# Four-layer hybrid encoder: a norm's squares summed on TensorE inside the first unit of the next stage

## The chip, the cores and the metric

The kernel runs on one core of a Trainium2 chip. The metric is the device time of one execution in microseconds (us). Shown of before are three runs and one profiled execution. The engines are named as the profile names them: PE is TensorE's matmul, PEld its weight load, DVE is VectorE, ACT is ScalarE, POOL is GpSimd, SP the queue that issues the weight transfers.

## The reference, cut to what matters

256 tokens of width 1024 pass four layers, each a mixer and an MLP, with a norm ahead of both and one at the end. The mixers are a state-space mixer (layers 0 and 3, called mix0 and mix3), a dilated attention (mix1) and a differential attention (mix2).

```python
def rmsnorm(x, g):
    y = x * rsqrt(mean(x * x, axis=-1, keepdims=True) + 1e-6)
    return y * g
for i in range(4):
    x = x + mixer[i](rmsnorm(x, norm_mix_g[i]), ...)
    h = rmsnorm(x, norm_mlp_g[i])
    x = x + square(relu(h @ mlp_w1[i])) @ mlp_w2[i]
out = rmsnorm(x, final_norm_g)
# differential attention, per head: softmax(a) - lambda * softmax(b), with
# lambda = exp(sum(l0 * l1)) - exp(sum(l2 * l3)) + lam_init
```

The factor of the norm, r = rsqrt(mean + eps), is one number per token; g is one number per channel. A projection of rmsnorm(x) is thus the projection of x * g, scaled by r for each token.

## The kernel before, in words

The activations lie transposed: `xT` has 8 tiles of 128 channels by 256 tokens. Every weight chunk (128 x 1024 numbers) comes by a transfer on SP into `raw`, is rounded by ACT (`whi`, line 110) and its rest taken by DVE (`wlo`, line 112). Activations are kept as such pairs too, and `mm3` (lines 149 to 151) makes each product of three matmuls: whi with the high part, whi with the low part, wlo with the high part. A "unit" is one projection of 256 columns: 48 matmuls of 128 x 256, in two halves of 24, one for each weight chunk.

At the end of a stage, `finish(n)` adds each of the eight finished tiles to `xT` (line 1151), and `norm_tile` makes the next stage's input of it: `norm_split` gives x * g as a pair (`uh`, `ul`; lines 232 and 233, tile `spl`), and `norm_square` squares the tile on ACT (lines 241 and 244). POOL adds the first seven squares to `sqacc` (line 246). `sums` (line 274) then adds over the channels by matmuls with one moving column (`guard`): the squares are the stationary operand, once for each half of the tokens, for `sqacc`, for the eighth square, and for a column of ones that carries eps. That is 6 products, and the trace shows each as two instructions, 12 in all. `rsqrt` is seven small DVE operations (lines 260 to 265); `bcast_tok` spreads r over a tile `rbc` (DVE line 282, a matmul, ACT line 284). All this is `norm_finish`.

`normalised` then multiplies `xT` by g and r and splits the result (`nf` or `nt`, `nh`, `nl`; lines 304 to 306), 8 tiles each.

Where the norm is used:
- The MLP works on `uh`, `ul` and scales by `rbc` as a unit leaves PSUM (line 349). `norm_finish("a3")` is written after `up(0)`, the first 96 matmuls.
- Each mixer calls `norm_finish("a0")` and `normalised` in `start`, ahead of its first unit. The first two units of mix0 and mix3, the first three q/k units of mix1 (`defer=3`) and the first q and k of mix2 work on `uh`, `ul` and are scaled behind (lines 460, 798, 983, tile `qkt`); all other units, the v chunks and `dt_unit` work on `nh`, `nl`.
- mix1's and mix2's `start` also clear key tiles by POOL (`kl`, line 136; lines 767, 772, 773), and mix2's `start` computes lambda (lines 943 to 951, with a matmul at line 945).
- `final` calls `sums` after everything else; PE has transposed the scaled output tiles (`final_tile`, line 1102) by then.

In `load` four pairs of squares are made by ACT (line 197) and added by DVE (line 201).

The order is set by a scheduler at build time: each engine has one fixed list, made from the order in which the program is written, priorities, and the scheduler's own idea of durations. The mixers write out their units by due times (`E(t, fn)`). `shifted("hi")` and `shifted("lo")` put the two conversions of a weight chunk back in priority by amounts set for each stage (`TUNE`).

Of the kernel before, what the change touches and what calls it, by code (L numbers as in the profile page):

```python
# [16 lines left out]
P = 128  # L17
# [7 lines left out]
NSPL = 12  # L25
NRAW = 5
CH = 1024
# [3 lines left out]
def classes(t):  # L31

    return t.rearrange("p (j c) -> p c j", c=4)

# [11 lines left out]
class Prog:  # L46
    def __init__(self, ctx, tc, aps, parts):
# [6 lines left out]
        self.ap_ = ep("small")  # L54
        self.sp = ep("sp")
# [77 lines left out]
    def lo_keys(self, name):  # L133

        t = self.lp.tile([P, 2, T], F32R, name=name)
        self.nc.gpsimd.memset(t[64:128].bitcast(F32), 0.0)
        return t

# [15 lines left out]
    def load(self, g, perm):  # L154
# [13 lines left out]
        for n, v in ((1, EPS / P), (D, 1.0 / D), (8 * D, 0.125 / D)):  # L168
            self.guard[n] = self.const.tile([P, 1], F32, name=f"guard{n}")
            nc.vector.memset(self.guard[n], v)  # L170
        self.ident = self.V("ident", 0, P)
# [22 lines left out]
        for c, b in enumerate(banks):  # L194
            nc.vector.tensor_copy(out=self.xT[:, 2 * c:2 * c + 2, :], in_=b)
            q = self.lp.tile([P, 2, T], F32, name=f"sq{c}")
            nc.scalar.activation(out=q, in_=b, func=AF.Square)
            if c == 0:
                sq = q
            else:  # L200
                nc.vector.tensor_tensor(out=sq, in0=sq, in1=q, op=ALU.add)
        self.sqs = [sq[:, 0, :], sq[:, 1, :]]
# [33 lines left out]
    def norm_square(self, j):  # L236
        nc = self.nc
        x = self.xT[:, j, :]
        if j == 0:
            self.sqs = [self.ap_.tile([P, T], F32, tag="sqacc", name="sqacc", bufs=2)]  # L240
            nc.scalar.activation(out=self.sqs[0], in_=x, func=AF.Square)
        else:
            sq = self.ap_.tile([P, T], F32, tag="sq", name="sq", bufs=3)
            nc.scalar.activation(out=sq, in_=x, func=AF.Square)  # L244
            if j < KD - 1:
                nc.gpsimd.tensor_tensor(out=self.sqs[0], in0=self.sqs[0], in1=sq, op=ALU.add)  # L246
            else:
                self.sqs.append(sq)

    def norm_tile(self, j, g, perm=False):  # L250
        if g is not None:
            self.norm_split(j, g, perm, self.xT[:, j, :])
        self.norm_square(j)

    def rsqrt(self, v, n):
# [3 lines left out]
        y, w, q = t("y"), t("w"), t("q", I32)  # L259
# [8 lines left out]

    def sums(self, bank, tiles, count):

        cols = [(self.ones, self.guard[1])] + [(t, self.guard[count]) for t in tiles]
        for i, (t, v) in enumerate(cols):
            for h in range(2):
                self.nc.tensor.matmul(bank[:, h:h + 1], lhsT=t[:, 0:P] if i == 0 else t[:, h * P:(h + 1) * P], rhs=v,
                                      start=i == 0 and h == 0, stop=i == len(cols) - 1, skip_group_check=True)

    def bcast_tok(self, r, scale, bank, out):
# [5 lines left out]
        nc.tensor.matmul(bank[:, 256:512], lhsT=self.ones, rhs=dg, start=True, stop=True)  # L283
        nc.scalar.copy(out=out, in_=bank[:, 256:512])

    def norm_finish(self, tag="r0"):
        nc = self.nc
        bank = self.bank(tag)
        self.sums(bank, self.sqs, D)
        r = self.rsqrt(bank[:, 0:2], 2)  # L290
        self.rbc = self.ap_.tile([P, T], F32, tag="rbc", name="rbc", bufs=2)
        self.bcast_tok(r, 1.0, bank, self.rbc)

    def normalised(self, g_mix, perm=False, keep=False):

        nc = self.nc
        nh, nl = (self.lp.tile([P, KD, T], F32R, name=n) for n in ("nh", "nl"))
        self.nf = self.lp.tile([P, KD, T], F32, name="nf") if keep else None
        rbc = classes(self.rbc) if perm else self.rbc
        for k in range(KD):  # L300
            x = classes(self.xT[:, k, :]) if perm else self.xT[:, k, :]
            t = self.nf[:, k, :] if keep else self.lp.tile([P, T], F32, tag="nt", name="nt", bufs=2)
            tv = t.rearrange("p (c j) -> p c j", c=4) if perm else t
            nc.vector.scalar_tensor_tensor(out=tv, in0=x, scalar=g_mix[:, k:k + 1], in1=rbc, op0=ALU.mult, op1=ALU.mult)
# [20 lines left out]
    def mlp(self, l, finish):  # L325
# [78 lines left out]
    def ssd_events(self, l, finish):  # L404
# [12 lines left out]
        def start():  # L417
            self.norm_finish("a0")
            st["n"] = self.normalised(gvec("g_mix", 8 * l, 8), keep=any(n[0] != "o" for n in cfg["native"]))
# [9 lines left out]
        def unit(kind, c0, defer):  # L429
# [227 lines left out]
        def r2():  # L657
            bank = self.bank("r2")

            self.sums(bank, [st["sq"][:, n, :] for n in range(2)], 8 * D)  # L660
            r = self.rsqrt(bank[:, 0:2], 2)
# [67 lines left out]

    def bias_rows(self):  # L730
# [19 lines left out]
    def dil_events(self, l, finish):  # L750
# [7 lines left out]
        cj = lambda t: t.rearrange("p (c j) -> p c j", c=4)  # L758

        def start():  # L760
            self.norm_finish("a0")
            st["rbp"] = lp.tile([P, T], F32, name="rbp")
            nc.scalar.copy(out=cj(st["rbp"]), in_=classes(self.rbc))
            st["n"] = self.normalised(self.V("g_mix", 8 * l, 8), perm=True)
            for i in range(2):
                st["bias", i] = lp.tile([P, 2, 514], F32, name=f"bias{i}")
                nc.gpsimd.memset(st["bias", i][:, :, 258:514], -1e30)
                st["kl", i] = self.lo_keys(f"kl{i}")
                for g in range(1, 3):
                    st["k", i, g] = [lp.tile([P, 2, T], F32R, name=f"k{i}{g}{q}") for q in range(2)]  # L770
                    for t in st["k", i, g]:
                        nc.gpsimd.memset(t[0:64, 1, :].bitcast(F32), 0.0)
                        nc.gpsimd.memset(t[64:128, 0, :].bitcast(F32), 0.0)
# [10 lines left out]
        def qk(hp, g, defer):  # L784
            b = self.bank(f"r{st.setdefault('rot', 0) % 2}")
            st["rot"] += 1
            nh, nl = (self.uh, self.ul) if defer else ([t[:, k, :] for k in range(KD)] for t in st["n"])
            for w in range(2):
                wh, wl = self.take((l, "qk", hp, g, w))
                o = b[:, w * T:(w + 1) * T]  # L790
                for k in range(KD):
                    c = slice(k * P, (k + 1) * P)
                    self.mm3(o, wh[:, c], wl[:, c], nh[k], nl[k], k == 0, k == 7)
                self.done()
            src = b.rearrange("p (w t) -> p w t", w=2)
            if defer:
                t = lp.tile([P, 2, T], F32, tag="qkt", name="qkt", bufs=2)
                nc.vector.tensor_tensor(out=t, in0=src, in1=st["rbp"].unsqueeze(1).to_broadcast([P, 2, T]), op=ALU.mult)
                src = t
# [17 lines left out]
        def vchunk(hp, i):  # L817
# [3 lines left out]
            nh, nl = st["n"]  # L821
# [450 lines left out]
```

## Time and profile before

| what | value |
|---|---|
| median of three runs | 1617.34 us (1616.33 to 1620.15) |
| the profiled execution | 1616.8 us, of which the span is 1615.0 us |
| PE busy | 1579.2 us (98%) |
| DVE, ACT, POOL busy | 1193.0, 959.2 and 133.1 us |
| mean transfer rate | 186 GB/s |

Stages by the trace, in us from the start of the span: load and the start of mix0 to about 45, mix0 to 245, mlp0 to 430, mix1 to 717, mlp1 to 900, mix2 to 1017, mlp2 to 1194, mix3 to 1426, mlp3 to 1606, the final norm to the end. [...]

### The profile page before, as it was taken

What the parts mean: (1) busy time and instruction counts of PE and PEld (TensorE: products, weight loads), DVE (VectorE), ACT (ScalarE), POOL (GpSimd) and SP (SyncE); (2) the same over time, 40 slices, a digit from 0 to 9 for tenths busy, and PEclk for the clock granted to TensorE, in tenths of its full rate; (3) what the DMA queues carried; (4) which work ended last, traced back from release to release, by engine and by line L of the source; (5) the groups of instructions that cost most, each with busy time, mean ns of one, the idle gap of its engine ahead of it and who ended that gap; (6) DMA issues with size and microseconds to landing.
All of it is one profiled execution on the core that took longest, in us unless ns stands there. A gap on an engine that the chain in (4) does not pass through costs nothing.

```text
span 1615.0 us, 32385 instructions
## 1 busy us (share of the span) xinstructions
PE 1579.2 (98%) x13018; PEld 1534.2 (95%) x13018; DVE 1193.0 (74%) x1996; ACT 959.2 (59%) x1627; POOL 133.1 (8%) x122
## 2 busy tenths in 40 slices
PE   8999999999999999999999999999999999999998
PEld 7989899999989999999999999999998898899997
DVE  6999998555776667666555899755578999985554
ACT  5577866444566666764444677644455777664444
POOL 0012131000200000010000100100010231310001
PEclk9999999999999999999999999999999999999999
DMA  6677765665565555546566575566656677656661
GB/s 210 216 217 235 218 198 177 214 212 188 150 172 166 166 158 168 161 132 200 184 186 190 157 216 151 173 197 191 191 161 183 211 219 226 214 176 190 193 194 65
DMA packets 230294, 299.84 MB, mean 186 GB/s; under 512 B 16496, under 2 KB 166256, under 8 KB 230144
## 3 DMA queue, kind: packets, MB, share of 16 engines
q1 hardware_dynamic: 209552, 262.51, 53.1%
q10 hardware_dynamic: 20592, 35.27, 7.6%
q8 instruction: 102, 1.67, 0.4%
q14 instruction: 48, 0.39, 0.1%
HBM read 296.41 MB, written 3.62 MB: 186 GB/s over the span
## 4 chain that ended last, share of the span: by engine, by line
PE 75%; DVE 13%; DMA 5%; ACT 3%; issue 2%; POOL 0%; SPq 0%; DVEq 0%; ACTq 0%; POOLq 0%
PE r L149 13%; PE r L151 13%; PE r L150 13%; PE a L149 8%; PE a L150 8%; PE a L151 8%; DVE wlo L112 3%; DMA raw<-in_ssd_in_w_dram 2%; PE r L147 2%; DMA bc<-scr 1%; PE a L829 1%; PE a L830 1%; PE a L828 1%; PE r L620 1%; ACT whi L110 1%
## 5 line engine op out<-in xcount | busy, mean ns | idle before, releaser
L112 DVE TENSOR_TENSOR wlo<-raw,whi 128x1024 fp32r<-128x1024 f32 (+1 forms) x490 | 591.3, 1214 | 301.6 <-ACT whi L110 299.9
L110 ACT CAST whi<-raw 128x1024 fp32r<-128x1024 f32 (+1 forms) x490 | 503.1, 1034 | 450.6 <-PE r L150 224.4
L151 PE MATMUL r<-spl,wlo 128*128 128x256 f32 x1248 | 352.1, 282 | 3.7 <-DVE wlo L112 3.7
L149 PE MATMUL r<-spl,whi 128*128 128x256 f32 x1248 | 353.5, 283 | 0.5 <-ACT whi L110 0.5
L150 PE MATMUL r<-spl,whi 128*128 128x256 f32 x1248 | 353.2, 283 | 0.4
L149 PE MATMUL r<-nh,whi 128*128 128x256 f32 (+1 forms) x1024 | 291.6, 285 | 6.7 <-DVE kl L142 3.2
L151 PE MATMUL r<-nh,wlo 128*128 128x256 f32 (+1 forms) x1024 | 286.9, 280 | 2.2 <-DVE wlo L112 2.2
L150 PE MATMUL r<-nl,whi 128*128 128x256 f32 (+1 forms) x1024 | 286.8, 280 | 0.0
L150 PE MATMUL a<-hl,whi 128*128 128x256 f32 x1024 | 286.0, 279 | 0.0
L149 PE MATMUL a<-hh,whi 128*128 128x256 f32 x1024 | 286.0, 279 | 0.0
L151 PE MATMUL a<-hh,wlo 128*128 128x256 f32 x1024 | 285.6, 279 | 0.0
L151 PEld LDWEIGHTS r<-spl,wlo 128*128 128x128 f32 x1248 | 238.5, 191 | 4.3 <-DVE wlo L112 4.1
L150 PEld LDWEIGHTS r<-spl,whi 128*128 128x128 f32 x1248 | 239.1, 192 | 1.3 <-DVE spl L233 1.1
L149 PEld LDWEIGHTS r<-spl,whi 128*128 128x128 f32 x1248 | 238.7, 191 | 1.1 <-ACT whi L110 0.7
L149 PEld LDWEIGHTS r<-nh,whi 128*128 128x128 f32 (+1 forms) x1024 | 193.4, 189 | 11.0 <-issue 6.1
L151 PEld LDWEIGHTS r<-nh,wlo 128*128 128x128 f32 (+1 forms) x1024 | 193.3, 189 | 3.2 <-DVE wlo L112 2.4
L150 PEld LDWEIGHTS r<-nl,whi 128*128 128x128 f32 (+1 forms) x1024 | 193.8, 189 | 0.7 <-DVE nl L306 0.2
L149 PEld LDWEIGHTS a<-hh,whi 128*128 128x128 f32 x1024 | 193.4, 189 | 0.2 <-ACT whi L110 0.2
L150 PEld LDWEIGHTS a<-hl,whi 128*128 128x128 f32 x1024 | 193.5, 189 | 0.0
L151 PEld LDWEIGHTS a<-hh,wlo 128*128 128x128 f32 x1024 | 192.4, 188 | 0.0
L246 POOL TENSOR_TENSOR sqacc<-sqacc,sq 128x256 f32<-128x256 f32 x48 | 43.3, 901 | 1100.8 <-ACT sq L244 1099.1
L595 ACT ACTIVATE e<-bc,tb 128x256 f32<-128x256 f32 (+1 forms) x256 | 95.5, 446 | 1.5 <-issue 1.5
(249 smaller groups left out, 2400.8 us busy)
## 6 DMA issues: line engine op xcount, KB each, us to landing
raw<-in_mlp_w_dram SPq DMA_DIRECT2D x256, 512.0 KB
raw<-in_ssd_in_w_dram SPq DMA_DIRECT2D x96, 512.0 KB
bc<-scr ACTq DMA_DIRECT2D x32, 768.0 KB
raw<-in_dil_qkv_w_dram SPq DMA_DIRECT2D x48, 512.0 KB
raw<-in_ssd_out_w_dram SPq DMA_DIRECT2D x32, 512.0 KB
raw<-in_dil_qkv_w_dram SPq DMA_DIRECT2D x64, 192.0 KB
raw<-in_diff_qkv_w_dram SPq DMA_DIRECT2D x24, 512.0 KB
raw<-in_dil_out_w_dram SPq DMA_DIRECT2D x8, 512.0 KB
```

Of the source, the lines that this page charges most:

```text
L110: self.nc.scalar.copy(out=hi[:, :n], in_=raw[:, :n])
L112: self.nc.vector.tensor_tensor(out=lo[:, :n], in0=raw[:, :n], in1=hi[:, :n].bitcast(F32), op=ALU.subtract)
L147: mm(out, lhsT=wh, rhs=xh, start=start, stop=stop, skip_group_check=True)
L149: mm(out, lhsT=wh, rhs=xh, start=start, stop=False, skip_group_check=True)
L150: mm(out, lhsT=wh, rhs=xl, start=False, stop=False, skip_group_check=True)
L151: mm(out, lhsT=wl, rhs=xh, start=False, stop=stop, skip_group_check=True)
L246: nc.gpsimd.tensor_tensor(out=self.sqs[0], in0=self.sqs[0], in1=sq, op=ALU.add)
L595: X = lambda o, i_, bias: nc.scalar.activation(out=o, in_=i_, func=AF.Exp, bias=bias)
L620: nc.tensor.matmul(b[(h % 2) * 64:(h % 2) * 64 + 64, n * T:(n + 1) * T], lhsT=xt[:, 1 - i, h * 64:(h + 1) * 64], rhs=G[h][:, i * T:(i + 1) ...
L828: mm(o, lhsT=nh[:, k, t], rhs=w_h, start=k == 0, stop=False)
L829: mm(o, lhsT=nh[:, k, t], rhs=w_l, start=False, stop=False)
L830: mm(o, lhsT=nl[:, k, t], rhs=w_h, start=False, stop=k == 7)
```

## The change

- `sums` loses the column of ones; eps is added by one more DVE operation on the two result columns. POOL's additions go: all eight squares go through `sums`, that is 16 products. Each of these matmuls is kept in program order, behind the PE instruction written before it; so is the matmul of `bcast_tok`.
- `norm_finish` is cut in two. `norm_sums` (matmuls and `rsqrt`) is written after the first 24 matmuls of a mixer's first unit, and after the first 48 of `up(0)` in an MLP; `norm_rows` (spreading r) after that unit.
- mix1 and mix2 have no `normalised` any more: all units work on `uh`, `ul`; q and k are multiplied by `rbc` as they leave PSUM, v by r with ACT's scale. mix0 and mix3 write `normalised` after the first unit; `dt_unit` works on `uh`, `ul`.
- Lambda is computed in mlp0, after the bias vectors. The key tiles are cleared within the first units.
- In `load`, squares are not added, and the conversions are not put back (`hi` and `lo` 0).
- `NSPL` goes from 12 to 16 (tiles for pairs), squares have 8 buffers for 3, a tile of 96 columns is left empty, the scratch for dynamic transfers is set to 4096.

```diff
     def sums(self, bank, tiles, count):
-        cols = [(self.ones, self.guard[1])] + [(t, self.guard[count]) for t in tiles]
-        for i, (t, v) in enumerate(cols):
+        for i, t in enumerate(tiles):
             for h in range(2):
-                self.nc.tensor.matmul(bank[:, h:h + 1], lhsT=t[:, 0:P] if i == 0 else t[:, h * P:(h + 1) * P], rhs=v, ...)
+                self.behind(self.nc.tensor.matmul(bank[:, h:h + 1], lhsT=t[:, h * P:(h + 1) * P], rhs=self.guard[count], ...))
+        v = self.ap_.tile([P, 2], F32, tag="ms", name="ms", bufs=2)
+        self.nc.vector.tensor_scalar(out=v, in0=bank[:, 0:2], scalar1=EPS, scalar2=None, op0=ALU.add)
+        return v
...
+    def behind(self, ins):
+        self.tc.keep_in_program_order(ins)
...
-    def norm_square(self, j):
+    def norm_square(self, j, perm):
         x = self.xT[:, j, :]
-            ...
-                nc.gpsimd.tensor_tensor(out=self.sqs[0], in0=self.sqs[0], in1=sq, op=ALU.add)
+        sq = self.ap_.tile([P, T], F32, tag="sq", name="sq", bufs=KD)
+        self.nc.scalar.activation(out=cj(sq) if perm else sq, in_=classes(x) if perm else x, func=AF.Square)
+        self.sqs.append(sq)
...
-    def norm_finish(self, tag="r0"):
+    def norm_sums(self, tag):
+        self.nbank = self.bank(tag)
+        self.r = self.rsqrt(self.sums(self.nbank, self.sqs, D), 2, "n")
+
+    def norm_rows(self):
+        self.rbc = self.ap_.tile([P, T], F32, tag="rbc", name="rbc", bufs=2)
+        self.bcast_tok(self.r, 1.0, self.nbank, self.rbc)
...
@@ mlp, up(s)
+                if s == 0 and j == 2:
+                    self.norm_sums("a3")
@@ mix0 and mix3, unit
                     self.done()
+                    if first and i == 0:
+                        self.norm_sums("a0")
+                if first:
+                    self.norm_rows()
                 evac(kind, c0, b.rearrange("p (n t) -> p n t", n=2), defer)
+                if first:
+                    st["n"] = self.normalised(gvec("g_mix", 8 * l, 8))
@@ mix1, qk
-            if defer:
-                t = lp.tile([P, 2, T], F32, tag="qkt", name="qkt", bufs=2)
-                nc.vector.tensor_tensor(out=t, in0=src, in1=st["rbp"]..., op=ALU.mult)
+                if first and w == 0:
+                    self.norm_sums("a0")
+                    fill(0)
+            if first:
+                self.norm_rows()
+            src = lp.tile([P, 2, T], F32, tag="qkt", name="qkt", bufs=2)
+            nc.vector.tensor_tensor(out=src, in0=b..., in1=self.rbc..., op=ALU.mult)
@@ final
-        self.sums(b, self.sqs, D)
-        r = self.rsqrt(b[:, 0:2], 2)
+        r = self.rsqrt(self.sums(b, self.sqs, D), 2)
```

More of the change, by code (lines that the diff above doesn't have):

```diff
@@ L24 @@
 NBUF = 5
-NSPL = 12
+NSPL = 16
 NRAW = 5
+GAP = 96
 CH = 1024
@@ L54, in __init__ @@
         self.ap_ = ep("small")
+        self.ap_.tile([P, GAP], F32, name="gap")
         self.sp = ep("sp")
@@ L167, in load @@
         self.guard = {}
-        for n, v in ((1, EPS / P), (D, 1.0 / D), (8 * D, 0.125 / D)):
+        for n, v in ((D, 1.0 / D), (8 * D, 0.125 / D)):
             self.guard[n] = self.const.tile([P, 1], F32, name=f"guard{n}")
             nc.vector.memset(self.guard[n], v)
+        self.lamt = self.const.tile([P, 6], F32, name="lamt")
         self.ident = self.V("ident", 0, P)
@@ L282, in bcast_tok, with normalised_tiles, normalised @@
             nc.vector.tensor_scalar(out=dg[:, b * P:(b + 1) * P], in0=self.ident, scalar1=r[:, b:b + 1], scalar2=scale, op0=ALU.mult, op1=ALU.mult)
-        nc.tensor.matmul(bank[:, 256:512], lhsT=self.ones, rhs=dg, start=True, stop=True)
+        self.behind(nc.tensor.matmul(bank[:, 256:512], lhsT=self.ones, rhs=dg, start=True, stop=True))
         nc.scalar.copy(out=out, in_=bank[:, 256:512])
-    def norm_finish(self, tag="r0"):
-        nc = self.nc
[L288 to L299, printed above, removed]
+    def norm_sums(self, tag):
[4 more added lines that the diff above has]
+        self.bcast_tok(self.r, 1.0, self.nbank, self.rbc)
+    def normalised_tiles(self, keep):
+        self.nhl = [self.lp.tile([P, KD, T], F32R, name=n) for n in ("nh", "nl")]
+        self.nf = self.lp.tile([P, KD, T], F32, name="nf") if keep else None
+    def normalised(self, g_mix):
+        nc = self.nc
+        nh, nl = self.nhl
         for k in range(KD):
[L301 to L304, printed above, removed]
+            t = self.nf[:, k, :] if self.nf is not None else self.lp.tile([P, T], F32, tag="nt", name="nt", bufs=2)
+            nc.vector.scalar_tensor_tensor(out=t, in0=self.xT[:, k, :], scalar=g_mix[:, k:k + 1], in1=self.rbc, op0=ALU.mult, op1=ALU.mult)
             nc.scalar.copy(out=nh[:, k, :], in_=t)
@@ L417, in start @@
         def start():
-            self.norm_finish("a0")
-            st["n"] = self.normalised(gvec("g_mix", 8 * l, 8), keep=any(n[0] != "o" for n in cfg["native"]))
+            self.normalised_tiles(any(n[0] != "o" for n in cfg["native"]))
             st["sq"] = lp.tile([P, 2, T], F32, name="sqy")
@@ L658, in r2 @@
             bank = self.bank("r2")
-            self.sums(bank, [st["sq"][:, n, :] for n in range(2)], 8 * D)
-            r = self.rsqrt(bank[:, 0:2], 2)
+            r = self.rsqrt(self.sums(bank, [st["sq"][:, n, :] for n in range(2)], 8 * D), 2)
             st["r2"] = lp.tile([P, T], F32, name="r2bc")
@@ L728, in bias_vectors, with lambdas @@
         nc.scalar.dma_start(out=self.bvec, in_=v)
+    def lambdas(self):
+        nc = self.nc
+        self.lam = []
+        for j in range(1):
+            lam_init = 0.8 - 0.6 * math.exp(-0.3 * (3 * j + 2))
+            t = self.lamt[:, 6 * j:6 * j + 6]
+            v = self.V("lam", 4 * j, 4).rearrange("p (a b) -> p a b", b=2)
+            nc.vector.tensor_tensor(out=t[:, 0:2], in0=v[:, :, 0], in1=v[:, :, 1], op=ALU.mult)
+            b = self.bank("r2")
+            nc.tensor.matmul(b[:, 0:2], lhsT=self.ones, rhs=t[:, 0:2], start=True, stop=True)
+            nc.scalar.activation(out=t[:, 2:4], in_=b[:, 0:2], func=AF.Exp)
+            nc.vector.scalar_tensor_tensor(out=t[:, 4:5], in0=t[:, 3:4], scalar=-lam_init, in1=t[:, 2:3], op0=ALU.add, op1=ALU.subtract)
+            nc.vector.tensor_scalar(out=t[:, 5:6], in0=self.V("subln", j), scalar1=1.0 - lam_init, scalar2=None, op0=ALU.mult)
+            self.lam.append((t[:, 4:5], t[:, 5:6]))
     def bias_rows(self):
@@ L782, in load_bias, with qk @@
                                         in_=self.slanted("four", 2 * hp + h, 64, [(256 - 1, 64), (128, 2), (1, 64)]))
-        def qk(hp, g, defer):
+        def qk(hp, g):
             b = self.bank(f"r{st.setdefault('rot', 0) % 2}")
             st["rot"] += 1
-            nh, nl = (self.uh, self.ul) if defer else ([t[:, k, :] for k in range(KD)] for t in st["n"])
+            first = hp == 0 and g == 0
             for w in range(2):
@@ L958, in load_bias, with proj @@
             st["bias", h] = bt
-        def proj(kind, p, defer):
-            nh, nl = (self.uh, self.ul) if defer else ([t[:, k, :] for k in range(KD)] for t in st["n"])
+        def proj(kind, p):
+            nh, nl = self.uh, self.ul
+            first = kind == "q" and p == 0
             b = self.bank({"q": "r0", "k": "r1", "v": "a0"}[kind])
@@ L1132, in run @@
                 self.bias_vectors()
+                self.lambdas()
                 self.bias_rows()
```

126 lines of the change are left out of this document (52 added, 74 removed).

## The prediction

> **What bounds the kernel now.** I read the page first, then PE's waits, then windows by stage, then the timeline around each norm.
>
> ```profile
> span 1615.0 us, 32385 instructions
> PE 1579.2 (98%) x13018; PEld 1534.2 (95%) x13018; DVE 1193.0 (74%) x1996; ACT 959.2 (59%) x1627; POOL 133.1 (8%) x122
> ```
> PE has work nearly all the time, and its weight loads are as full as its matmuls. What more PE is given costs time, unless it falls into a gap. The windows by stage (length, then busy time and count of PE, PEld, DVE, ACT and POOL, then clock, DMA share, GB/s) are those of mix1, mlp1, a stretch of up-matmuls, and mix3:
>
> ```profile
> 465.00:690.00 225.00, 221.76 (x1817) 217.17 (x1816) 155.45 (x341) 149.95 (x263) 0.00 (x0) 0.99 0.60 169
> 735.00:890.00 155.00, 155.00 (x1318) 155.00 (x1317) 87.20 (x87) 73.81 (x87) 0.00 (x0) 1.00 0.60 185
> 1017.00:1028.00 11.00, 11.00 (x100) 11.00 (x99) 10.96 (x15) 8.08 (x16) 5.47 (x6) 1.00 0.43 127
> 1240.00:1415.00 175.00, 168.55 (x1317) 154.50 (x1316) 169.22 (x240) 129.11 (x257) 43.91 (x23) 1.00 0.72 223
> ```
> In the MLPs PE never stands; one matmul takes 11.00 / 100 = 0.11 us. In mix3 DVE is as full as PE. Mix1 leaves DVE 70 us free. So the change must pay by gaps; these are PE's:
>
> ```profile
> PE r L151 <- DVE wlo L112: 5.8, 2, 3.7
> PE a L274 <- POOL sqacc L246: 4.5, 3, 2.4
> PE r L149 <- DVE kl L142: 3.2, 1, 3.2
> PE a L945 <- DVE lamt L951: 1.5, 1, 1.5
> PE a L283 <- DVE dg L282: 1.3, 2, 0.6
> ```
> (total us, times, longest). Behind a long gap the clock falls too. Stretches of 3.41 us, laid where the granted clock changes:
>
> ```profile
> 902.87:906.28 3.41, 2.51 (x20) 2.31 (x20) 3.08 (x7) 1.58 (x5) 2.32 (x5) 1.00 0.48 150
> 906.28:909.70 3.42, 3.42 (x17) 3.42 (x18) 2.57 (x11) 1.04 (x1) 0.00 (x0) 0.50 0.79 260
> 1196.42:1199.83 3.41, 1.59 (x14) 1.59 (x15) 2.48 (x5) 1.34 (x5) 1.14 (x1) 1.00 0.65 188
> 1199.83:1203.25 3.42, 3.42 (x18) 3.42 (x18) 2.70 (x10) 1.04 (x1) 0.00 (x0) 0.50 0.31 108
> 1247.62:1251.03 3.41, 1.90 (x16) 1.67 (x16) 3.41 (x8) 2.00 (x3) 1.24 (x1) 1.00 1.10 358
> 1251.03:1254.45 3.42, 3.42 (x26) 3.26 (x25) 3.42 (x8) 3.42 (x11) 0.00 (x0) 1.00 1.00 302
> 728.79:732.20 3.41, 3.41 (x32) 3.41 (x32) 1.77 (x6) 1.04 (x1) 0.00 (x0) 1.00 0.89 332
> 732.20:735.62 3.42, 3.42 (x28) 3.26 (x27) 2.32 (x7) 1.32 (x2) 0.00 (x0) 1.00 0.63 190
> ```
> and of the first, third and seventh of them the matmuls of `sums` alone:
>
> ```profile
> 902.87:906.28 3.41, 0.78 (x7) 0.81 (x7) 1.00 0.48 150
> 1196.42:1199.83 3.41, 1.10 (x8) 1.05 (x8) 1.00 0.65 188
> 728.79:732.20 3.41, 1.40 (x12) 1.37 (x12) 1.00 0.89 332
> ```
> The stretch from 902.87 has PE busy for 2.51 us and is followed by half clock; that from 1247.62 has 1.90 and is not. Busy time doesn't part them. Full-width matmuls do: 20 - 7, less lambda's 2 = 11 (1.2 us) before half clock, 14 - 8 = 6 before half clock, 16 and 32 - 12 = 20 without. I read it so: a matmul with one moving column does not count as activity, and a stretch with too few full-width ones sets the clock to half for the next 3.41 us. The bound lies between 11 and 16 of them; I take 1.3 us, near its lower end, which is the kinder to the change. A stretch at half clock takes 17 or 18 matmuls instead of 31: 13.5 x 0.11 = 1.5 us lost.
>
> **The change part by part.** *The sums.* Their price now, at the start of mlp1:
>
> ```profile
> 728.85 0.50 PE L274 MATMUL a<-guard,ones 128*128 128x1 f32 x4
> 729.22 0.59 PE L274 MATMUL a<-guard,sqacc 128*128 128x1 f32 x4
> 729.66 0.59 PE L274 MATMUL a<-guard,sq 128*128 128x1 f32 x4
> 730.11 0.36 PE L149 MATMUL r<-spl,whi 128*128 128x256 f32 x1
> ```
> 12 instructions in 730.11 - 728.85 = 1.26 us, 0.105 each, as much as a full matmul, since each has weights of its own. After the change there are 32, or 3.36 us: 2.1 us more for each of 8 norms within the stream, **+16.8**. Mix0's and mix3's inner norms go from 12 to 8: **-0.8**. None hides in the MLPs.
>
> *The clock.* 3.36 us of one-column matmuls in one block nearly fill a stretch of 3.41. The clock falls if some stretch holds more than 3.41 - 1.3 = 2.1 us of the block; it stays only if both parts are under 2.1, so the cut must lie in 0.8 us of 3.41: three in four fall. I take 0.6, since late squares may space the block. Mix0 and mix1 have such stretches already (below), so six norms: 6 x 0.6 x 1.5 = **+5.4**; ends 0 and 9.0. [...]
>
> *The end.* Now DVE's `rs_q` waits for the sums alone, which the scheduler put ahead of the last transposes (line 1102):
>
> ```profile
> 1607.48 0.42 PE L1102 MATMUL r<-head,yT 128*128 128x128 f32 x2
> 1607.65 0.16 DVE L260 TENSOR_SCALAR rs_q<-a 128x2 int32<-128x2 int32 x1 [1.31 <-PE a L274]
> ```
> Pinned, they start behind those at 1607.9 and end 3.36 later; with 0.17 to DVE (1607.48 to 1607.65) and 0.16 for the added operation (as long as `rs_q`), `rs_q` comes at 1611.6 instead of 1607.65: +4.0. Nothing covers it; the output waits for it. At half clock a sum costs double (8 took 1.87 us in the load's row below); a third of them so, +1.0: **+5.0**, ends 4.0 and 7.4.
>
> *The load.*
>
> ```profile
> 19.05 0.58 PE L151 MATMUL r<-spl,wlo 128*128 128x256 f32 x1 [3.66 <-DVE wlo L112]
> 19.65 1.87 PE L274 MATMUL a<-guard,sq 128*128 128x1 f32 x8
> 15.41:18.82 3.41, 0.00 (x0) 0.00 (x0) 3.27 (x5) 3.30 (x6) 0.00 (x0) 1.00 0.42 161
> 18.82:22.23 3.41, 3.18 (x14) 3.09 (x15) 2.05 (x6) 0.00 (x0) 0.00 (x0) 0.50 0.52 152
> 22.23:25.65 3.42, 3.42 (x18) 3.42 (x18) 3.35 (x8) 0.00 (x0) 0.00 (x0) 0.50 0.84 232
> L201 DVE TENSOR_TENSOR sq<-sq,sq x3: 684/693/694, 15.7 to 18.9; 128x512 f32<-128x512 f32 x3
> ```
> The awaited `wlo` stood in DVE's list behind additions that go (0.69 each), and is no longer put back. The wait of 3.7 goes and one of two half-clock stretches: **-5.2**; ends 0 (the eight squares on ACT are late next) and -6.7.
>
> *Mix1's start* waits for POOL's last addition, but the last split pair comes no earlier:
>
> ```profile
> 434.39 1.59 DVE L233 SCALAR_TENSOR_TENSOR spl<-xT,head,spl 128x256 fp32r<-128x256 f32 x2
> 435.64 1.01 PE L274 MATMUL a<-guard,sqacc 128*128 128x1 f32 x4 [2.41 <-POOL sqacc L246]
> 435.25:438.66 3.41, 3.02 (x14) 3.02 (x15) 1.14 (x4) 0.00 (x0) 3.06 (x9) 0.50 0.45 127
> ```
> All 24 matmuls of the first half need it (to 435.98), and the sums stand behind them: **0**; -5.4 (2.4 and two half-clock stretches) if the second half's matmuls are put in between.
>
> *Mix2's and mix3's starts.* Here the first half needs only four tiles, and the sums run while the last come. Mix2 loses lambda's wait (1.5) and 0.2 for sqacc, mix3 its 1.9 (4.5 - 2.4 - 0.2), both one half-clock stretch: **-3.2 and -3.4**. If lambda's cover in mlp0 were gone it would cost its two matmuls, 0.2. *The MLPs* lose the waits for `dg`: **-1.3**.
>
> *Scaling q and k.* The wait of 3.2 for `kl` in mix1 is a PSUM bank held until q and k are split by ACT and DVE in turn; after, one DVE operation frees it:
>
> ```profile
> 476.21:479.62 3.41, 0.19 (x1) 0.22 (x2) 2.77 (x5) 3.08 (x7) 0.00 (x0) 1.00 0.48 138
> 479.62:483.03 3.41, 3.41 (x17) 3.41 (x17) 2.34 (x5) 2.05 (x5) 0.00 (x0) 0.50 0.68 191
> L798 DVE TENSOR_TENSOR qkt<-r,rbp x3: 677/681/685, 444.4 to 458.1; 128x512 f32<-128x512 f32 x3
> ```
> The wait and its half clock: **-4.7**, end 0. The operation comes 27 times more (21 in mix1, 6 in mix2), 18.4 us of DVE, hidden by the 70 free; uncovered, up to that. What `normalised` did in mix1 and mix2 is off PE's path (0). The v scaling and `dt_unit` replace operations one for one, 0; if not, an operation under 0.7 each. POOL's clears move behind the first half; no engine waits for them among the rows above, 0, and some 3 us (POOL's busy time from 435.25) for the first `kl` if they come late. Buffers and the empty tile: no row, 0, with the width of the range.
>
> Sum: 16.8 - 0.8 + 5.4 + 5.0 = 26.4 against 5.2 + 3.2 + 3.4 + 1.3 + 4.7 = 17.8: +8.6 on the profiled execution's 1616.8, or **1625**; the median shown is 0.5 above that execution.
>
> **The rivals.** *The clock stays up* (weight loads count, or the scheduler mixes the sums among other matmuls): without 5.4 and the tail's 1.0 it is 1616.8 + 2.2 = 1619, no change. For it: 12 sums at 728.79 did no harm. Against: the two stretches above. [...]
>
> *Faster: the sums fall into the gaps.* In mix0 and mix1 PE stands for 3.7 and 2.4 us while the last tiles come; if the sums of the earlier squares run there, 2 x 2.1 less is paid; with all waits regained (6.7 + 5.4 + 3.2 + 3.4 + 1.3 + 4.7 = 24.7) and the clock kept: 16.8 - 4.2 - 0.8 + 4.0 - 24.7 = -8.9, 1608. It decides once the regained time passes what is paid, 15.8, by 3.2. Against: the pins, and mix1's last split.
>
> *Slower still: the waits only change their name.* If the load, mix1's bank and mix3 keep theirs (late squares on ACT, DVE's 27 more operations), 5.2 + 4.7 + 3.4 = 13.3 less is regained: 1639.
>
> **How the numbers follow.** Forecast 0.53, clock stays 0.20, faster 0.14, waits stay 0.13. A measurement here tells 0.2%, 3.2 us, from no change. Faster is 0.14 and a part of the second case, 0.17; same the rest of it and the forecast's edge, 0.22; slower 0.61. The range reaches from within the faster case, 1610, to short of the slowest, 1633; the forecast's own is 1620 to 1632.
>
> **What the changed profile would show.** L274-like sums 32 in a row in 3.4 us in each MLP; behind most of them a stretch of 3.41 us with clock 0.50; `rs_q` of the end some 3.7 us after the last transposes. No wait for POOL or lambda, none for `kl` in mix1's second pair. Wrong would be the forecast if the MLPs' starts keep a clock of 1.00, or if the sums stand apart from each other.

## The result: 22 us slower, more than twice the forecast

| | before | after |
|---|---|---|
| median | 1616.84 us (4 runs) | 1639.12 us (1635.24 to 1640.73, 4 runs) |
| profiled execution, span | 1616.8, 1615.0 us | 1638.78, 1636.9 us |

The ratio is 1.0135, 95% interval [1.0114, 1.0155]. The forecast was 1625, at most 1633: the direction was right, the size was not. Medians and ratios, here and below, leave out single runs over 1.5% above the fastest of the same kernel; that concerns three runs, the longest 5664.91 us. The page of the changed kernel begins

```profile
span 1636.9 us, 32647 instructions
PE 1609.9 (98%) x13190; PEld 1566.7 (96%) x13190; DVE 1182.8 (72%) x2000; ACT 958.4 (59%) x1616; POOL 89.5 (5%) x74
```
PE has 172 instructions and 30.7 us of busy time more; POOL lost 43.6 of its 133.1 us. To place the difference I cut both traces at the first and last down-matmul of each MLP. The windows between (columns as in the prediction: length, then busy time and count of PE, PEld, DVE, ACT, POOL, then clock, DMA share, GB/s) are load, mix0 and mlp0's first unit; mix1 and mlp1's first unit; mix2 and mlp2's; mix3 and mlp3's; the end. Before:

```profile
0.00:270.50 270.50, 261.37 (x2004) 243.69 (x2005) 247.34 (x413) 180.58 (x345) 42.07 (x33) 0.98 0.69 212
430.06:742.11 312.05, 305.74 (x2496) 299.12 (x2495) 219.93 (x457) 200.24 (x350) 15.50 (x29) 0.98 0.57 161
900.28:1041.49 141.21, 137.89 (x1170) 136.09 (x1169) 125.49 (x355) 98.37 (x218) 10.09 (x13) 0.99 0.58 174
1193.69:1451.12 257.43, 247.72 (x1952) 230.88 (x1950) 241.75 (x396) 172.94 (x334) 51.98 (x31) 0.99 0.65 201
1605.61:1615.00 9.39, 2.23 (x19) 1.79 (x17) 2.94 (x10) 2.36 (x5) 0.73 (x1) 0.70 0.30 112
```
After:

```profile
0.00:271.97 271.97, 264.14 (x2040) 247.08 (x2041) 244.67 (x415) 180.41 (x348) 37.98 (x27) 0.99 0.68 211
431.72:743.22 311.50, 310.10 (x2535) 303.69 (x2534) 223.10 (x464) 199.81 (x342) 6.99 (x20) 0.98 0.57 161
901.40:1048.64 147.24, 145.80 (x1208) 144.31 (x1206) 118.20 (x343) 96.61 (x210) 0.99 (x2) 0.97 0.55 164
1200.84:1463.45 262.61, 254.82 (x1988) 238.71 (x1986) 238.74 (x400) 172.71 (x331) 42.50 (x23) 0.98 0.65 196
1623.40:1636.86 13.46, 4.94 (x39) 4.42 (x37) 3.12 (x11) 2.30 (x5) 0.00 (x0) 0.69 0.21 78
```
The windows sum to +16.2 (1.47 - 0.55 + 6.03 + 5.18 + 4.07). The rest is in the MLPs between them, 5.5 of it in mlp3, where nothing was edited. Two stretches of 120 us inside mlp0 and mlp2 of the changed kernel show what that is:

```profile
300.00:420.00 120.00, 120.00 (x1021) 120.00 (x1021) 65.41 (x64) 53.95 (x62) 0.00 (x0) 1.00 0.66 204
1060.00:1180.00 120.00, 120.00 (x1062) 120.00 (x1061) 67.59 (x66) 56.64 (x65) 0.00 (x0) 1.00 0.64 194
```
Full clock, no wait, the same instructions, and yet 1021 or 1062 of them: 117.5 ns or 113.0 ns each. From the start of one dense matmul (128 x 256, right behind another) to the start of the next it is 117.8 ("wide") or 113.3 ns ("narrow"), mostly for a whole MLP, and worth 6 us of it. In this pair of profiles before had two wide MLPs and after three.

### The profile page after: what moved, and what is told of

Read it like the earlier page. It is cut to its first block, busy times and chain, and to the rows that moved or that the text cites. A ratio compares the mean times of both kernels' runs of the same rounds, so it can differ in the third digit from the quotient of the medians.

```text
span 1636.9 us, 32647 instructions
## 1 busy us (share of the span) xinstructions
PE 1609.9 (98%) x13190; PEld 1566.7 (96%) x13190; DVE 1182.8 (72%) x2000; ACT 958.4 (59%) x1616; POOL 89.5 (5%) x74
## 4 chain that ended last, share of the span: by engine, by line
PE 81%; DVE 11%; ACT 4%; DMA 2%; issue 2%; POOL 0%; ACTq 0%; DVEq 0%; POOLq 0%; SPq 0%
PE r L150 14%; PE r L151 14%; PE r L152 14%; PE a L150 8%; PE a L152 8%; PE a L151 8%; DVE wlo L119 3%; PE a L271 2%; PE r L148 2%; DMA bc<-scr 1%; PE a L856 1%; PE a L854 1%; PE a L855 1%; ACT whi L117 1%; DVE cvx L486 1%
## 5 line engine op out<-in xcount | busy, mean ns | idle before, releaser
L150 PE MATMUL r<-spl,whi 128*128 128x256 f32 x1696 | 480.7, 284 | 0.9 <-ACT spl L233 0.9
L151 PE MATMUL r<-spl,whi 128*128 128x256 f32 x1696 | 478.4, 282 | 0.5 <-DVE spl L234 0.3
L152 PE MATMUL r<-spl,wlo 128*128 128x256 f32 x1696 | 477.6, 282 | 0.0
L150 PEld LDWEIGHTS r<-spl,whi 128*128 128x128 f32 x1696 | 323.2, 191 | 1.7 <-ACT spl L233 1.1
L151 PEld LDWEIGHTS r<-spl,whi 128*128 128x128 f32 x1696 | 322.5, 190 | 1.3 <-DVE spl L234 1.1
L152 PEld LDWEIGHTS r<-spl,wlo 128*128 128x128 f32 x1696 | 322.4, 190 | 0.4 <-DVE wlo L119 0.2
L150 PE MATMUL r<-nh,whi 128*128 128x256 f32 x576 | 164.5, 286 | 7.0 <-DVE cvx L486 3.4
L151 PE MATMUL r<-nl,whi 128*128 128x256 f32 x576 | 161.0, 280 | 0.4 <-DVE nl L308 0.4
L152 PE MATMUL r<-nh,wlo 128*128 128x256 f32 x576 | 161.2, 280 | 0.2 <-DVE wlo L119 0.2
L150 PEld LDWEIGHTS r<-nh,whi 128*128 128x128 f32 x576 | 109.1, 189 | 10.7 <-DVE cvx L486 3.6
L152 PEld LDWEIGHTS r<-nh,wlo 128*128 128x128 f32 x576 | 109.0, 189 | 1.2 <-DVE wlo L119 0.8
L151 PEld LDWEIGHTS r<-nl,whi 128*128 128x128 f32 x576 | 109.0, 189 | 0.9 <-DVE nl L308 0.6
```

Source lines behind the costliest of these rows:

```text
L150: mm(out, lhsT=wh, rhs=xh, start=start, stop=False, skip_group_check=True)
L151: mm(out, lhsT=wh, rhs=xl, start=False, stop=False, skip_group_check=True)
L152: mm(out, lhsT=wl, rhs=xh, start=False, stop=stop, skip_group_check=True)
```

## The experiments

**Is the spacing chance, or the change's doing?** Each kernel once more, unedited, and ten MLPs in a row with either norm:

```diff
-ALL = [f"{k}{l}" for l in range(DEPTH) for k in ("mix", "mlp")] + ["final"]
+ALL = [f"mlp{i % 4}" for i in range(10)] + ["final"]
```


> The changed kernel once more, nothing edited. Two theories on the spacing of dense matmuls in the MLPs (113.3 or 117.8 ns for a whole MLP, 5.5 us of an MLP's 155). A: it falls by chance in each execution; then the pattern of the first profile (mlp0, mlp1 and mlp3 at the wide spacing, mlp2 at the narrow one) is not repeated in all four, and the part of the difference put down to mlp3 belongs to no edit. B: it is set by the kernel; the same pattern comes back.

> The kernel before once more, nothing edited. Chance: the spacing of the MLPs' matmuls differs from the first profile's (mlp0 and mlp1 wide, mlp2 and mlp3 narrow) in at least one. Set by the kernel: the same pattern, and a span within 1 us of 1615.0.

> The kernel before with its list of stages replaced by ten MLPs in a row and the final norm; the mixers are left out, so the output is another. It gives ten starts of an MLP and ten draws of the spacing in one execution. Expected: no half-clock stretch at any start (in two profiles of the whole kernel none of 8), and wide and narrow MLPs mixed if the spacing is chance; two of eight were wide so far.

Measured: the changed kernel 1636.15 against 1612.35 for the runs of before beside it, ratio 1.0131 [1.0058, 1.0205]: the 22 us stand. But mlp0 was narrow now and mlp1, mlp2, mlp3 wide; before had all four narrow, and a span of 1598.4. Of the ten MLPs, four were wide with the old norm and four with the new. So it fell anew in each of these executions, and ten draws each show no favour for either kernel. From start of sums to start of sums in the ten MLPs of before, a narrow and a wide one:

```profile
553.57:729.72 176.15, 176.15 (x1553) 175.90 (x1551) 108.27 (x121) 89.31 (x113) 5.61 (x6) 1.00 0.59 192
729.72:912.58 182.86, 182.85 (x1553) 182.60 (x1552) 108.97 (x121) 89.35 (x113) 5.78 (x6) 1.00 0.57 186
```
One draw is worth 6.7 us, and runs of before went from 1600 to 1625. From here on I compare profiles at equal spacing too: 4.5 ns (117.8 - 113.3) are taken off for each pair of neighbouring dense matmuls 115.6 to 120.6 ns apart. Three spans of before, 1615.0, 1598.4 and 1620.6, are then 1595.0, 1590.5 and 1593.4 (the third is the run with an unused constant, below): the spacing made most of the spread. After is 1609.4 and 1616.8: **+20.1**.

**What a norm costs.**

> The changed kernel, ten MLPs and the final norm. Forecast by the prediction's terms for each of the ten starts: 20 more instructions x 0.105 = 2.1, 0.6 half-clock stretches x 1.5 = 0.9, the wait for dg gone 0.6: 2.3 more than the other ten-MLP kernel, at equal spacing. Half clock at 5 to 7 of the ten starts by the theory that one-column matmuls are no activity; at none by the rival that weight loads keep the clock. Spacing: if it is chance, about as many wide MLPs as in the other kernel; if the change favours the wide one (6 of 8 against 2 of 8 so far), 7 or more of ten against 4 or fewer, which would be up to 12 us of the whole kernel's difference.

The same window for three MLPs with the new norm, a wide one without half clock and two narrow ones with one and two stretches of it:

```profile
748.86:933.77 184.91, 184.91 (x1572) 184.86 (x1571) 106.50 (x122) 89.23 (x113) 0.00 (x0) 1.00 0.56 183
201.33:381.06 179.73, 179.73 (x1572) 179.68 (x1571) 105.94 (x122) 89.42 (x113) 0.00 (x0) 0.99 0.57 188
1120.19:1301.53 181.34, 181.34 (x1572) 181.29 (x1571) 105.94 (x122) 89.42 (x113) 0.00 (x0) 0.98 0.57 186
```
The sums alone cost 184.91 - 182.86 = 2.05, as forecast. The clock costs 179.73 - 176.15 - 2.05 = 1.5 for one stretch, 3.1 for two. None of before's nine inner starts (from one MLP to the next) fell, that is had half clock behind it; of the new norm's nine, two had none, four one and three two: 10 stretches, 1.1 per start where I took 0.6. A start with two, in stretches of 3.41 us, first everything, then `sums` alone:

```profile
1119.52:1122.93 3.41, 3.41 (x34) 3.41 (x32) 0.27 (x1) 1.04 (x1) 0.00 (x0) 1.00 0.60 180
1122.93:1126.34 3.41, 3.41 (x17) 3.41 (x18) 1.69 (x5) 0.00 (x0) 0.00 (x0) 0.50 0.02 7
1126.34:1129.76 3.42, 3.42 (x18) 3.42 (x18) 1.14 (x7) 0.05 (x1) 0.00 (x0) 0.50 0.49 153
```
```profile
1119.52:1122.93 3.41, 2.74 (x26) 2.86 (x26) 1.00 0.60 180
1122.93:1126.34 3.41, 1.58 (x8) 1.50 (x8) 0.50 0.02 7
```
(A count takes in what reaches over a boundary.) In the first, PE is busy all of 3.41 us, but only 34 - 26 = 8 matmuls are full-width, that is have 256 moving columns: the next stretch runs at half clock. There the remaining 8 sums take double time (1.58 us, 0.20 each) and leave room for 17 - 8 = 9 full-width ones: the one after falls too. That second fall I had not counted. The start without half clock had 33 - 19 = 14 and 31 - 15 = 16:

```profile
747.46:750.88 3.42, 3.42 (x33) 3.42 (x32) 1.00 (x1) 1.04 (x1) 0.00 (x0) 1.00 0.71 225
750.88:754.29 3.41, 3.41 (x31) 3.41 (x31) 1.66 (x5) 0.00 (x0) 0.00 (x0) 1.00 0.09 37
```
```profile
747.46:750.88 3.42, 2.02 (x19) 2.13 (x20) 1.00 0.71 225
750.88:754.29 3.41, 1.60 (x15) 1.52 (x14) 1.00 0.09 37
```
Another block's stretch, from 559.73, fell with 34 - 22 = 12. So the bound, which I had between 11 and 16, lies above 12 and at most at 14 in these stretches. The twenty profiles agree: of 134 stretches at full clock with half clock behind them, every one held at most 13 matmuls with more than one moving column, though PE was busy for over 3.3 us in 39 of them; of 9552 that kept the clock, all but four held 14 or more. In the first profile of the changed kernel the starts of mlp0, mlp1 and mlp3 kept their clock, in the second all three fell.

The block spread out, one product behind each three matmuls:

```diff
-                if s == 0 and j == 2:
-                    self.norm_sums("a3")
...
+                        if s == 0 and j in (1, 2):
+                            self.norm_product(8 * (j - 1) + 4 * kk + n)
```


> Ten MLPs with the changed norm (the mixers are left out), the 16 products of the sums spread out: one behind each three matmuls of the second and third chunk. By the theory (a stretch falls when it holds too few full-width matmuls) no stretch has under 2.0 us of them, so no half clock at any of the nine inner starts, and 178.0 us from start to start, as where the block of 32 kept its clock. Rival (the half clock comes from the weight loads or the waits around the norm): 5 or more of nine starts fall as with the block.

No stretch at half clock at any inner start. A stretch amid the sums has 33 - 12 = 21 full-width matmuls (everything, then the sums' line alone):

```profile
744.41:923.06 178.65, 178.43 (x1572) 178.18 (x1571) 105.93 (x123) 89.66 (x114) 0.00 (x0) 1.00 0.58 189
746.00:749.41 3.41, 3.41 (x33) 3.41 (x32) 0.51 (x1) 0.90 (x1) 0.00 (x0) 1.00 0.65 209
```
```profile
746.00:749.41 3.41, 1.66 (x12) 1.81 (x13) 1.00 0.65 209
```
It takes 178.65, where I had expected 178.0: 178.65 - 176.15 = 2.5, 0.45 more than the sums in a block that kept its clock (a wait of 0.2 for `dg` among it). With as many matmuls and weight loads from start to start (1572 and 1571 with either order), none of nine starts fell where 7 of 9 did with the block: here the half clock came with the block, not with waits or weight loads, as the theory had it.

**The sums and the pins in the whole kernel.** POOL's additions back at the ends of stages, and the pins off:

```diff
-        sq = ...(tag="sq", bufs=KD); ...; self.sqs.append(sq)
+        if j == 0 or j == KD - 1: self.sqs.append(sq)
+        else: nc.gpsimd.tensor_tensor(out=self.sqs[0], in0=self.sqs[0], in1=sq, op=ALU.add)
```


> The changed kernel with POOL's additions put back at the ends of the stages: the first seven squares are added on POOL, two tiles of squares go through the sums (4 products, 8 instructions) in the new places; the load, the pins and the scaled projections stay. Theory (the sums' own instructions and the half clock behind them are the cost): 7 norms x 24 instructions x 0.105 us = 17.6 us less, and the half-clock stretches at the starts of mix2, mlp2 and mix3 and at the end go (4 x 1.5 = 6); waits for POOL come back at the starts of mix1, mix2, mix3 and at the end (1 to 2.4 each). Together 17 to 22 us below the changed kernel, 1617 to 1622. Rival 1 (the scaling of the attention projections and the new order cost it): within 5 us of the changed kernel, 1634 or more. Rival 2 (dense matmuls of the MLPs run at one of two spacings, and the change set mlp3 to the slower): mlp3 is 5.5 us shorter or not, whatever the sums do.

```diff
     def behind(self, ins):
-        self.tc.keep_in_program_order(ins)
+        pass
```


> The changed kernel without the pins: the scheduler may place the sums and the spreading matmul. By the built order only two places differ: at mix1's start the sums come six matmuls earlier and the spreading matmul later, and at the end the sums stand ahead of the last pair of transposes. Theory (the instructions cost, not where they stand): 0 to 1 us less than the changed kernel. Rival (the pins cost: the end and mix0's inner norm): 4 us or more below the changed kernel.

POOL's additions: 1620.29, ratio to before 1.0052 [1.0015, 1.0088]. The time lies among the 1617 to 1622 forecast, but before had 1612.35 beside it: by the ratios about 13 us of the 21 go, not 17 to 22. At equal spacing mix1 and mix2's windows are 301.9 and 140.1, below before's (307.1 and 141.2 on average), but mix0's and mix3's are 276.7 and 262.7, 8 above; PE waits 8.8 for `sqacc`, 4.5 in before. Without pins: 1625.73, ratio 1.0083 [1.005, 1.0116]. That is 10 us below the changed kernel beside it (1636.15), as the rival had it, but the intervals overlap, and the changed kernel's own runs went from 1624.70 to 1645.84. The edit moves two places. The end is 12.0 for 13.3. At mix1's start the block comes six matmuls earlier, ahead of a stretch at half clock, and takes 3.78 us where both profiles of the changed kernel have 6.82:

```profile
434.42 3.78 PE L271 MATMUL a<-guard,sq 128*128 128x1 f32 x32
```
So in this one profile the pins are worth some 4 us. Whether that is more than a draw stays open.

**The scaling alone.** The changed kernel with load, POOL's additions, order of the sums and mix0's and mix3's `normalised` as before; left are the scaled projections, lambda, the later clears, and `dt_unit` on `uh`, `ul`.

> The scaling of the attention projections as they leave PSUM, lambda in the first MLP and the later clears of key tiles alone; the load, POOL's additions, the column of ones, the order of the sums and the mixers' normalised tiles are as in the kernel before. By the prediction's terms: mix1's wait for kl and its half clock go, 4.7, and mix2 loses lambda's wait, 1.5 to 3.0: 6 to 8 us faster than before, about 1605. Rival (27 more DVE operations cost in mix1 and mix2): no faster than before, or up to 10 slower.

It took 1656.09, ratio 1.0259 [1.0218, 1.03], and its dense matmuls were spaced 118.7 ns in every stage. One constant more had moved all tiles behind it by 32 bytes.

> The kernel with the scaling of the attention projections alone, once more, with its weight and activation tiles at the addresses of the changed kernel, 32 bytes modulo 64 (in the run before a constant more had moved them to 0 modulo 64, and every dense matmul, in mix0 too where nothing was edited, was spaced 118.7 ns). Theory (the address set that spacing): 113.3 or 117.8 ns again, and by the prediction's terms 5 to 8 us faster than before. Rival 1 (the scaling itself slows the kernel): 1650 again. Rival 2 (27 more DVE operations eat the gain): within 3 us of before.

> The kernel before with one more constant of 32 bytes that nothing uses, so that all tiles behind it lie at 0 modulo 64 and not at 32. If the address sets the spacing: 118.7 ns in every stage, all MLPs 7 to 8 us longer than at 113.3, about 1650. If not: 1612 as before.

My theory of the address fell twice: at the old addresses it still took 1657.24 (1.0263), and before moved by 32 bytes took 1612.67, ratio 0.9993 [0.9961, 1.0025]. What both slow kernels shared was the distance between weight tiles (`whi`, `wlo`) and activation tiles (`spl`, `hh`, `hl`): the tile `ms` (64 bytes) was missing between them. In the built programs the first `spl` lies behind the first `whi` by 64 modulo 128 in before (102880 - 52512 = 50368) and after (94176 - 40224 = 53952), by 0 in those two (50816). An empty tile moves the activation tiles and what lies behind them, and leaves the weights:

```diff
         self.ap_ = ep("small")
+        self.ap_.tile([P, 8], F32, name="pad2")    # 8, 16 or 32 columns of 4 bytes
```


> Ten MLPs of the kernel before (mixers left out), with the activation tiles (the moving operand) at 0 modulo 64 and the weights still at 32. If the moving operand's address sets the wide spacing: 118.7 ns throughout, 1813 + about 60. If the weights' address does: 113.3 and 117.8 mixed as before. If it is both together: a third value, possibly the narrow one in all ten.

> Ten MLPs of the kernel before (mixers left out), activation tiles 64 bytes further from the weights (distance 0 modulo 128). Theory: 118.7 ns in every MLP, 184 us from start to start. Rival (something else in the two kernels with the scaling alone slowed them): 113.3 and 117.8 as before.

> Ten MLPs of the kernel before (mixers left out), activation tiles 128 bytes further from the weights (distance 64 modulo 128 still, 320 modulo 512 for 192). If the period is 128: 113.3 and 117.8 mixed, 176.2 and 182.9 us from start to start. If a longer period counts: one spacing throughout, narrow or wide.

One MLP of the first two and two of the third, distances 96, 0 and (twice) 64 modulo 128:

```profile
575.72:759.39 183.67, 183.67 (x1552) 183.53 (x1551) 109.00 (x121) 89.24 (x113) 5.81 (x6) 1.00 0.56 184
```
```profile
583.07:769.25 186.18, 186.18 (x1552) 186.07 (x1551) 109.31 (x121) 89.02 (x113) 5.87 (x6) 1.00 0.56 182
```
```profile
208.00:384.14 176.14, 176.14 (x1552) 175.98 (x1551) 108.25 (x121) 89.20 (x113) 5.62 (x6) 1.00 0.59 191
384.14:566.99 182.85, 182.85 (x1553) 182.69 (x1552) 108.99 (x121) 88.98 (x113) 5.80 (x6) 1.00 0.56 186
```
At 96 all MLPs take 183.7 (118.3 ns), at 0 all take 186.2 (120.0 ns, where I had expected 118.7), at 64 they are drawn between the two known values, also with 128 more. The address of the moving tiles alone, the first choice of the run at 96, is excluded: before moved by 32 bytes has them at 0 modulo 64 too, and took 1612.67. So in these four the spacings went with the distance, and 128 bytes more left both values (176.14 and 182.85 us) as they were; why, no run shows. With it put right the scaling could be read:

> The kernel with the scaling alone (as in the run before), with an empty tile of 64 bytes ahead of the activation tiles: they then lie at the same distance from the weight tiles, modulo 128 and 512, as in the kernels before and after (64 and 192; in the run at 1657 the distance was 0 and 128). Theory (the distance sets the spacing): 113.3 or 117.8 ns again, and 5 to 8 us faster than before by the prediction's terms for kl and lambda. Rival 1 (the scaling slows every matmul): 1650 to 1660 again. Rival 2 (the distance is the cause, but the gain of the scaling is eaten by DVE's added work): within 3 us of before.

1629.23, ratio 1.0142 [1.0113, 1.0172]: the wide 118.7 is gone, the gain isn't there. At equal spacing mix1 is 302.3, 4.8 shorter, as forecast (4.7); but mix0 is 277.4 for 268.3 and mix3 260.0 for 254.7, though of the edits only `dt_unit` stands there.

**dt_unit.** Put back in three surroundings:

```diff
-                self.mm3(b[0:64, 0:T], wh[:, c], wl[:, c], self.uh[k], self.ul[k], k == 0, k == 7)
+                self.mm3(b[0:64, 0:T], wh[:, c], wl[:, c], nh[:, k, :], nl[:, k, :], k == 0, k == 7)
...
-            nc.vector.tensor_tensor(out=sb, in0=b[0:64, 0:T], in1=self.rbc[0:64, :], op=ALU.mult)
+            nc.scalar.copy(out=sb, in_=b[0:64, 0:T])
```


> The scaling alone, with dt_unit on nh and nl and copied by ACT as in the kernel before. Theory (dt_unit on u with its scaling on DVE is what cost in mix0 and mix3): mix0 and mix3 as in the kernel before, 268 and 254 us at the narrow spacing, mix1 4 us shorter; in all 3 to 6 us faster than before. Rival (the cost comes from elsewhere: the order that the scheduler makes of all of it): mix0 still 5 us or more longer, in all 10 or more slower than before.

> The changed kernel with dt_unit alone put back. If dt_unit's scaling costs: mix3 4 to 6 us and mix0 2 to 4 us shorter than in the changed kernel, in all 1628 to 1632. Rival (in the changed kernel nh and nl come later, so dt_unit waits for them and the conv rows come later still): no gain, or some us slower.

> The changed kernel with POOL's additions and dt_unit both put back. By the terms read so far: the kernel with POOL's additions had mix1 5 and mix2 1 us shorter than before, the end 1 longer, mix0 and mix3 8 longer each. If dt_unit was the cause of the latter: 2 to 5 us faster than before. If not: 6 to 9 slower, as it was.

With the scaling alone it was the cause: 1608.74, ratio 1.0008 [0.9983, 1.0034], mix0 266.6 and mix3 254.7. The 3 to 6 us faster that I expected did not show in the time. PE's wait for `cvx` (total, times, longest) in the kernel with `dt_unit` on `uh`, and DVE's wait ahead of it in mix0:

```profile
PE r L151 <- DVE cvx L496: 10.6, 3, 5.2
```
```profile
DVE bc L590 <- DMA bc<-scr: 6.8, 3, 3.6
```
and with it put back:

```profile
PE r L151 <- DVE cvx L496: 1.1, 2, 0.9
```
```profile
DVE bc L591 <- DMA bc<-scr: 2.4, 3, 1.0
```
DVE stands in its list at an addition to `bc` until the transfer of the rows has landed, and `cvx` is queued behind it. Moving `dt_unit` moved that chain. In the changed kernel the same edit gives nothing: 1629.01 lies among the 1628 to 1632 that I expected, but before had 1609.35 beside it, the ratio is 1.014 [1.0111, 1.0169], and mix0 (272.8) and mix3 (262.6) are no shorter. Beside POOL's additions it is 1.0045 [1.0025, 1.0066] for 1.0052; there its one profile has mix0 at 269.4 for 276.7, 7.3 shorter (4.6 of that half clock), and mix3 still at 262.1. So the 0 that I gave `dt_unit` holds for the changed kernel, but not where the rest is as before; that the order made by the scheduler decides it is my reading, not shown. Nor does the old place of the norm help:

> The changed kernel with the norm of mix0 and mix3 (sums, spreading, normalised tiles) written in start again, ahead of the first unit and without pins there; the 32 sums stay. Theory (in mix3 the later normalised tiles push DVE's work into the body: the wait for cvx of 3.1 to 3.8 us and two half-clock stretches behind it): mix3 4 to 7 us shorter than in the changed kernel, mix0 2 shorter. Rival (the sums alone make mix3 longer): both as long as in the changed kernel within 1.5 us.

1629.84, ratio 1.0141 [1.0073, 1.0208]; mix0 274.1 for 269.9 in the changed kernel, mix3 262.3 for 261.6. That theory fell. Of all versions the scaling with the old `dt_unit` is the best, and it is level with before.

## Why the prediction was wrong

By windows, at equal spacing, mean of three profiles of before and two of after. The forecast is the prediction's terms put to their windows (2.1 for each block of sums, 0.9 for its half clock, 1.5 for each stretch that was to vanish, 0.3 for each wait for `dg`). "Half clock" is the time by which matmuls inside the stretches with granted clock 0.50 exceed their spacing at full clock.

| window | forecast | measured | half clock, forecast | half clock, measured |
|---|---|---|---|---|
| load, mix0, mlp0's start | -0.8 | 268.3 to 269.9: +1.6 | -0.6 | 5.2 to 3.2: -2.0 |
| mix1, mlp1's start | +0.1 | 307.1 to 310.0: +2.9 | -0.6 | 4.3 to 6.7: +2.4 |
| mix2, mlp2's start | +2.5 | 141.2 to 145.9: +4.7 | +0.3 | 2.8 to 4.9: +2.1 |
| mix3, mlp3's start | +1.9 | 254.7 to 261.6: +6.9 | +0.3 | 2.6 to 6.5: +3.9 |
| the end | +5.0 | 9.3 to 13.3: +4.0 | +1.0 | within the 4.0 |

- **The clock is the step that failed.** Its net was -0.6 in the first four windows (+5.4 for the new blocks, -6.0 for four stretches that were to vanish with their waits); measured is +6.4. That is 7.0 of the 11.4 missed. That stretches with few full-width matmuls have half clock behind them was borne out (at most 13 in all 134); what it would cost was wrong in three places.
  - A block costs 1.1 stretches, not 0.6: in the ten MLPs 7 of 9 starts fell, near the three in four that I had worked out and then lowered, and three of the seven fell twice. In the two profiles of the whole changed kernel the six blocks have 4 and 8 stretches.
  - Mix1's block I had put at 0, because its place has half clock anyway. But there all 32 sums run at half clock (the row below), 6.8 us in both profiles where the sum has 3.36, and the half clock grows from two stretches (in all three profiles of before) to three and four.
  - In mix3 stretches came up where the sum had none: three profiles of before have its half clock at 1199.83, at 1354.56, and at 1204.37 with 1378.45; each of the two of after has one at the start and two in the body (at 1259.81 and 1382.69 in the first). I had summed the stretches of one trace as if they were fixed to their places.

```profile
437.85 6.82 PE L271 MATMUL a<-guard,sq 128*128 128x1 f32 x32
```
- **The load's gain** was taken back in mix0, the second failure: 3.8 beside the clock (2.4 missed, though the clock gave 1.4 more than forecast). The wait of 3.7 for `wlo` is gone; PE's waits in the changed kernel show what came instead, `nh` for the third unit (the later `normalised`) and the squares of the inner norm:

```profile
PE r L150 <- DVE cvx L486: 3.4, 2, 3.1
PE a L152 <- DVE wlo L119: 2.8, 1, 2.8
PE r L150 <- ACT nh L307: 1.9, 1, 1.9
PE r L271 <- POOL sqy L644: 1.6, 1, 1.6
```
(The second row, in mix3, is no news: before has 2.5 there.) "What is late next" I had answered for the load with the squares on ACT alone. The first row, in mix3, is the same failure on a smaller scale: the prediction's stretch from 1247.62 kept its clock with 16 matmuls around a shorter wait for `cvx`; now the wait is 3.1 long, and half clock follows at 1259.81. These causes are read from the waits alone: with the norm written early again (above) neither mix0 nor mix3 was shorter, so what makes `nh`, the squares and `cvx` late stays open.
- **The sums**, +16.8: right (2.05 measured for 2.1).
- **The end**, +5.0: 4.07 and 3.8, near the lower end. `rs_q` came 4.2 after the sums began; their last part was at half clock:

```profile
1625.03 0.44 PE L1123 MATMUL r<-head,yT 128*128 128x128 f32 x2 [0.92 <-ACT yT L1121]
1625.31 3.96 PE L271 MATMUL a<-guard,sq 128*128 128x1 f32 x32
...
1629.50 0.17 DVE L254 TENSOR_SCALAR rs_q<-ms 128x2 int32<-128x2 int32 x1
```
- **The scaled projections**, -4.7: the wait for `kl` is gone and mix1 without the block of 32 sums is 4.8 to 6.1 shorter. Right in size, though `kl` itself is 3.2, 1.8 and 1.9 in three profiles of before: I had read the largest.
- **Mix2's and mix3's waits** for POOL and lambda are gone, as said. Beside the clock mix2's window grew by 2.6 where 2.2 was forecast, mix3's by 3.0 where 1.6 was.
- **The rivals.** "The clock stays up" is refuted by the stretch from 1119.52 (PE busy for 3.41 us, clock 0.50 behind it). "The waits only change their name" gave 1639, the time that came, but by luck: its mechanism explains the 3.8 in mix0 and at most the 1.4 in mix3, and the clock, which it left as forecast, made 7.0.
- **The spacing** was in no term. That it shifts the mean is not shown (four wide of ten with either norm); it makes 1616.8, the execution I summed against, one draw among 1600 to 1625.

## What to carry to other kernels

Where PE never stood, one-column matmuls with their own weights cost nearly as much as full ones here (0.105 us for 0.113 to 0.118), and a stretch with 26 of them beside 8 full ones had half clock behind it, one with 12 beside 21 had not: spread them among full-width ones, or leave the additions to an engine with time to spare (with POOL's the ratio to before was 1.0052 for 1.0131). The half-clock stretches of one trace came at other places in the next (in mix3 of three profiles of before at 1199.83; at 1354.56; at 1204.37 and 1378.45): take their number over several profiles before summing what goes away. And before an edit that adds or drops a small tile is judged, look whether the spacing of dense matmuls moved in stages that it doesn't touch (here to 118.7 ns, which cost 1.0263 of before's time for 1.0142).

## What the runs showed of the hardware

In the ten MLPs with the new norm, stretches of 3.41 us in which PE was busy throughout had half clock behind them with 8 or 12 matmuls of 256 columns beside 26 or 22 of one column, and full clock with 14 beside 19. At mix1's start a block of 32 one-column matmuls took 6.82 us at half clock in the changed kernel, and 3.78 us where most of it had the full clock (without pins).

Dense fp32r matmuls of 128 x 256 with their own weights ran at one of several spacings in these runs: 113.3 or 117.8 ns, changing from profile to profile, where the activation tiles lay 64 bytes (modulo 128) from the weight tiles; 118.3 ns at 96 (ten MLPs); 118.7 ns (the scaling alone) or 120.0 ns (ten MLPs) at 0. From 113.3 to 120.0 is 6%; in the whole kernel an empty tile of 64 bytes took the scaling alone from 1.0263 to 1.0142 of before's time. All tiles of before moved by 32 bytes left its time as it was (ratio 0.9993). The distance 32 wasn't tried, and other tiles may have a part in it. What draws between narrow and wide stays open. In mlp0 four small matmuls for the bias vectors break the row (from 301.38 in the scaling alone with the empty tile), and there the spacing changed in 5 of 12 profiles, in that one from 113.3 to 117.8.
